# An input projection of which five indices of the convolution side are multiplied in Strassen pairs

## The chip, the cores and the metric

The kernel runs on one core of one Trainium2 chip. The metric is the time of one execution on the device in microseconds (us). Before the change it is 1025.28 us, the median of three runs (1023.85 to 1026.14).

## The reference, cut to what matters

A block with two branches that read the same normalised input (512 tokens after 16 meta tokens, 2048 wide):

```python
hn = _rmsnorm(h_res, norm_in_g[l])
P = hn @ w_in[l]                       # 2048 x (4224 + 4096)
Pr, Pc = P[..., :RW_COLS], P[..., RW_COLS:]
...
y = _rwkv7_recurrence(rh, decay, kh, vh, kk, kk * ah)      # 16 tokens, then chunks of 64
...
Bg = Pc[..., 0 * D_CONV:1 * D_CONV]
Cg = Pc[..., 1 * D_CONV:2 * D_CONV]
hc = Pc[..., 2 * D_CONV:3 * D_CONV]
g_c = Pc[..., 3 * D_CONV:4 * D_CONV]
y_b = Bg * _causal_depthwise_conv(Cg * hc, conv_w[l]) * jax.nn.silu(g_c)
mix = jnp.concatenate([y_a, y_b], axis=-1)
h_res = h_res + mix @ w_out[l]
...
out = _rmsnorm(h_res, norm_f_g)
```

All is float32. The convolution is causal, three tokens wide, so a half of the tokens needs two tokens of the half before it.

## The kernel before, in words

**Tiles.** The input projection has 65 column tiles of 128: r, k, v and g (eight indices each), one low-rank tile, and on the convolution side B, C, h and gc (eight indices each). The tokens are in the columns of the matmuls: the input stands in SBUF as `xh` and `xl`, 16 blocks of 128 rows (depth) by 528 tokens, a rounded part and its remainder. Each block of weights is split the same way, and a product is three matmuls: rounded weights by both input parts, and the weights' remainder by the rounded input (`steps`, L305 to L317). Tiles r, g, C and h are done in two banks of 258 and 256 tokens, k and v in two of 264, B and gc in one of 512.

**Weights.** A tile's weights come as two halves of 512 KB (128 by 1024, depth 0 to 1023 and 1024 to 2047). `prefetch` (L128) loads a half on SP's queue into one of three raw buffers and splits it in two quarters (`split_w`, L121): ACT casts (L124), then DVE subtracts for the even quarter and POOL for the odd one (L125). There are six buffers for quarters, so up to three halves are split ahead of PE.

**Order.** PE's order is written out by hand. The list `plan` gives the order of the projection's tiles; `mains` is a generator that yields a matmul at a time, and `fill(ns)` (L529) takes as many from it as its argument covers by their columns. The arguments are the planner's costs `FW`. The other engines' instructions are ordered by the tile framework by priority. `later(ns, fn)` holds a transfer back until so much projection has been issued.

**Stages.** For each two of the eight pairs of heads, a couple (`prepare` twice, then `invert`), PE does low-rank, Gram and inversion matmuls with `fill` between them; the inversion's small triangular solve goes through DRAM and back. Operands of the recurrence are stashed in DRAM. Then `recur` (L918) goes through nine chunks; each loads its operands (`load_chunk`, L909: eight tiles `ct` of 288 KB per chunk, two chunks buffered) and has three fills, `p`, `u` and `s`. The rest of the projection is used up by these fills and those of the mixing after them. The last stage, from about 860 us, is the output projection; it is already done in Strassen form, and there sums of weights are made by transfers that add to their destination, issued by POOL (`add_by_transfer`, L1177).

**The convolution side before.** `use` (L379) empties the banks by DVE (`scaled`, L331: product times the token's scale `rs`), multiplies C and h on POOL, convolves (ACT and DVE), multiplies by B on POOL and gates by gc.

Of the kernel before, what the change touches and what calls it, by code (L numbers as in the profile page):

```python
# [27 lines left out]
NPAIR = 8  # L28
ALPHA = -0.3032653298563167
# [14 lines left out]
    evac=34, start=1062, lora=2200, gram=8000, gram_b=13500, gram2=5500, misc=2000, v=2000, vt=1000, solve=24500, solve_first=30000,  # L44
    tr=3200, lev=3000, cp=4200, out=1500, begin=19500, p=2900, u=2900, s=5200, last=3700, mix=2600,
# [3 lines left out]
AHEAD, WEIGHTS = 6000, 3000  # L49

# [26 lines left out]
def hymba_kernel(ctx: ExitStack, tc: tile.TileContext, xt, xtok, front, w_in, w_out, pv, lup, cst, msk, gf, out):  # L77
# [16 lines left out]
    yd = dp.tile([2 * NPAIR * CH, SEQ], F32, tag="yd", name="yd", bufs=1)  # L94
    mixd = {j: dp.tile([P, SEQ], F32, tag=f"mixd{j}", name=f"mixd{j}", bufs=1) for j in range(NPAIR, KT)}

# [7 lines left out]
    stream = []  # L104
    plan = [("lora", 0), ("k", 0), ("r", 0), ("B", 0), ("v", 0), ("k", 1), ("r", 1), ("v", 1), ("g", 0), ("g", 1)]
    for j in range(0, NPAIR, 2):
        if j:
            plan += [(what, i) for i in (j, j + 1) for what in ("k", "r", "v")] + [("g", j), ("g", j + 1)]
        plan += [(what, j // 2) for what in ("C", "h", "B", "gc") if j or what != "B"]
    plan += [(what, i) for i in range(4, NPAIR) for what in ("C", "h", "B", "gc")]  # L110
    tile_of = {"r": 0, "k": 8, "v": 16, "g": 24, "lora": 32, "B": 33, "C": 41, "h": 49, "gc": 57}
    for what, i in plan:
        m = tile_of[what] + i
        stream += [w_in[m, :, 0:1024], w_in[m, :, 1024:2048]]
    stream[0:8] = [stream[j] for j in (0, 2, 4, 6, 1, 3, 5, 7)]
    N_IN = len(stream)
    stream += [w_out[0, g] for g in range(3)]
    quarters, chain, low = {}, {}, {}
    state = {"next": 0}
# [7 lines left out]

    def prefetch(upto):  # L128
        while state["next"] < min(upto, len(stream) if chain else N_IN):
            j = state["next"]  # L130
            raw = chain[j - N_IN] if j >= N_IN else wp.tile([P, 1024], F32, tag="raw", name=f"wr{j}", bufs=3)
            state["dma"] = nc.sync.dma_start(raw, stream[j]).ins
            with tc.high_priority(offset=WEIGHTS):
                for q in range(2):
                    split_w(2 * j + q, raw[:, q * 512 : (q + 1) * 512], nc.gpsimd if q and 10 < j < N_IN else nc.vector)
            state["next"] = j + 1

# [8 lines left out]
    la = xp.tile([P, 2, L], F32R, name="la")  # L146
    ones = xp.tile([P, P + 2], F32R, name="ones")
    omm = xp.tile([P, 33], F32, name="omm")
    hv = xp.tile([P, 6, 8], F32, name="hv")
    hl = cp.tile([P, 2, 8], F32, name="hl")  # L150
    smask = xp.tile([P, NCH, CH], F32, name="smask")
# [6 lines left out]
    tp = ph1.enter_context(tc.tile_pool(name="tp", bufs=1))  # L158

# [3 lines left out]
    def tm(name):  # L163
        return tp.tile([P, LP], F32, tag="tm", name=name, bufs=3)
# [4 lines left out]
    cold = tp.tile([P, 512], F32, tag="tm", name="cold", bufs=3)  # L169
# [35 lines left out]
    def load_w(n, tag):  # L205
        t = view(tag, 512)
        nc.sync.dma_start(t, stream[n][:, 512:1024])
        return t
# [113 lines left out]
    def main(j, ranges, name):  # L322
        prefetch(2 * j + 4)
        ps = banks(ranges, name, pm, "main")
        for k4 in range(4):
            if k4 == 1:
                prefetch(2 * j + 5)
            yield from steps(ps, ranges, k4, 4 * j + k4)
        return ps

# [4 lines left out]
    def shift_full(ps, m, name, dst):  # L335
        pr = tp.tile([P, L + 1], F32, tag="pr", name=f"pr_{name}", bufs=2)
        nc.gpsimd.memset(pr[:, 0:1], 0.0)
        scaled(FULL, ps, pr, -1)
        sh = tm(f"sh_{name}")[:, 0:L]
        nc.scalar.activation(sh, pr[:, 0:L], AF.Copy, scale=col(V_MU, m))  # L340
        for (a, b), d in dst:
            nc.vector.scalar_tensor_tensor(
                out=d, in0=pr[:, a + 1 : b + 1], scalar=omm[:, m : m + 1], in1=sh[:, a:b], op0=ALU.mult, op1=ALU.add
            )

    def shift_real(ps, m, name, dst):
        pr = tp.tile([P, L + 1], F32, tag="pr", name=f"pr_{name}", bufs=2)
# [10 lines left out]
    def gate(g, name):  # L358
        th = tm(f"th_{name}")[:, 0:SEQ]
# [19 lines left out]
    def use(what, i, ps):  # L379
# [18 lines left out]
        elif what == "h":  # L398
# [6 lines left out]
            cv = tp.tile([P, SEQ], F32, tag="cw", name=f"cv{i}")  # L405
# [6 lines left out]
            if i == 0:  # L412
                nc.gpsimd.tensor_tensor(out=cv, in0=cv, in1=got["B", 0], op=ALU.mult)
        elif what == "B":
            b = tm(f"b{i}")[:, 0:SEQ] if i else tp.tile([P, SEQ], F32, name="b0")
            with behind_of("split"):
                scaled(REAL, ps, b, META)
            got[what, i] = b
            if i:
# [15 lines left out]
    def token_scale_sums():  # L435
# [3 lines left out]
        var = tp.tile([P, 3, 8], F32, tag="nv", name="var0")  # L439
# [20 lines left out]
    def mains():  # L460
# [35 lines left out]
        for j in range(4, len(plan)):  # L496
            what, i = plan[j]
            rg = FULL if what in ("k", "v") else REAL if what in ("B", "gc") else TAIL
            ps = yield from main(j, rg, f"{what}{i}")
            if what == "B" and i < 4:  # L500
                state["split"] = low[4 * j + 4]
# [542 lines left out]
    ph2.close()  # L1044
    with tc.tile_pool(name="ch", bufs=1, side="right", reuse_waits="tile") as ch:
        recur(ch)

# [72 lines left out]
    prefetch(len(stream))  # L1120
# [50 lines left out]
    def request(half, k, col, g):  # L1171
        t = wp.tile([P, 1024], F32, tag="raw", name=f"wo{half}{k}{col}{g}", bufs=3)
# [323 lines left out]
```

## Time and profile before

| | |
|---|---|
| median of three runs | 1025.28 us |
| span of the profiled execution, first to last instruction | 1023.6 us |
| PE, matmul busy | 1006.6 us, 98% of the span |
| DVE, ACT, POOL busy | 67%, 38%, 27% |
| transfers | 174.82 MB, a mean of 171 GB/s |

The page gives the busy time of each engine, the span in 40 slices, the transfer queues (q1 is what SP issues, q0 what POOL issues), the chain of work that ended last, and the costliest groups of instructions. A group's row has the line, the engine, the operation, output and inputs, then the busy time and the mean ns of one, then the idle time of the engine before it and what ended it. A row of waits says who waited for whom: us in total, times, longest. Matmuls are pipelined, and each is recorded with its whole latency, so what a matmul costs PE is read from the time between starts, not from its own duration. A share of a transfer queue is the time that its packets took on 16 engines, in parts of the window.

### The profile page before, as it was taken

How to read it: one execution, taken by the hardware profiler on the slowest of the kernel's cores; microseconds unless marked ns; L12 is line 12 of the kernel's file. 1: busy time of each engine (PE TensorE's matmuls, PEld its weight loads, DVE VectorE, ACT ScalarE, POOL GpSimd, SP SyncE). 2: the span in 40 equal slices, each digit the busy share in tenths (PEclk: the TensorE clock that was granted, in tenths of full speed). 3: DMA queues.
4: the chain of work that ended last, by engine and by line, in shares of the span. 5: the costliest groups of instructions: out<-in, count | busy, mean ns of one | idle time of the engine just before them, and what ended most of it. 6: DMA issues, size and time to landing. Idle time of an engine off the chain costs nothing.

```text
span 1023.6 us, 23708 instructions
## 1 busy us (share of the span) xinstructions
PE 1006.6 (98%) x9723; PEld 919.0 (90%) x9723; DVE 686.1 (67%) x1239; ACT 393.8 (38%) x729; POOL 273.8 (27%) x292
## 2 busy tenths in 40 slices
PE   9999999999999999999999999999999999999996
PEld 8899998999988999998999998889889897787885
DVE  7677954587765569654669653244555697998787
ACT  7553423344313434322434322222222335445453
POOL 0122323233332323232322232123332332015001
PEclk9999999999999999999999999999999999999999
DMA  9526476546764364864263845867673688695754
GB/s 333 152 63 148 122 190 182 150 123 143 167 172 134 96 170 99 217 167 117 83 166 98 220 139 168 309 212 235 195 232 93 183 276 192 172 319 135 172 125 165
DMA packets 185036, 174.82 MB, mean 171 GB/s; under 512 B 121568, under 2 KB 142816, under 8 KB 184416
## 3 DMA queue, kind: packets, MB, share of 16 engines
q1 hardware_dynamic: 182336, 164.40, 55.8%
q0 software_dynamic: 2304, 8.39, 4.7%
q8 instruction: 76, 1.25, 0.5%
q10 hardware_dynamic: 288, 0.52, 0.1%
q14 instruction: 32, 0.26, 0.1%
HBM read 136.92 MB, written 36.35 MB: 169 GB/s over the span
## 4 chain that ended last, share of the span: by engine, by line
PE 68%; DVE 8%; DMA 4%; issue 2%; SPq 1%; ACT 1%; POOL 0%; DVEq 0%; ACTq 0%; POOLq 0%
PE ps_gc L314 8%; PE ps_h L314 8%; PE ps_B L314 7%; PE ps_k L314 7%; PE ps_v L314 7%; PE ps_C L314 7%; PE ps_g L314 7%; PE ps_r L314 7%; DVE ol L1193 3%; DMA wo<-in_w_out_dram 2%; PE M L1220 2%; PE g L659 1%; PE zs L984 1%; PE Q L1220 1%; DVE xb L1201 1%
## 5 line engine op out<-in xcount | busy, mean ns | idle before, releaser
L125 POOL TENSOR_TENSOR wl<-wr,wh 128x512 fp32r<-128x512 f32 x119 | 169.2, 1423 | 370.8 <-ACT wh L124 356.4
L124 ACT CAST wh<-wr 128x512 fp32r<-128x512 f32 x252 | 152.7, 618 | 294.8 <-PE ps_C L314 51.9
L125 DVE TENSOR_TENSOR wl<-wr,wh 128x512 fp32r<-128x512 f32 x133 | 100.9, 765 | 109.0 <-ACT wh L124 108.6
L314 PE MATMUL ps_k<-xh,wl 128*128 128x264 f32 x256 | 73.1, 286 | 1.1 <-DVE wl L125 1.1
L314 PE MATMUL ps_v<-xh,wh 128*128 128x264 f32 x256 | 73.0, 285 | 0.0
L314 PE MATMUL ps_h<-xh,wh 128*128 128x258 f32 (+1 forms) x256 | 72.8, 284 | 0.0
L314 PE MATMUL ps_k<-xh,wh 128*128 128x264 f32 x256 | 72.8, 284 | 0.0
L314 PE MATMUL ps_v<-xl,wh 128*128 128x264 f32 x256 | 72.7, 284 | 0.0
L314 PE MATMUL ps_v<-xh,wl 128*128 128x264 f32 x256 | 72.7, 284 | 0.0
L314 PE MATMUL ps_k<-xl,wh 128*128 128x264 f32 x256 | 72.6, 284 | 0.0
L314 PE MATMUL ps_C<-xh,wh 128*128 128x258 f32 (+1 forms) x256 | 72.6, 284 | 0.0
L314 PE MATMUL ps_h<-xh,wl 128*128 128x258 f32 (+1 forms) x256 | 72.3, 282 | 0.2 <-issue 0.2
L314 PE MATMUL ps_r<-xh,wh 128*128 128x258 f32 (+1 forms) x256 | 72.4, 283 | 0.0
L314 PE MATMUL ps_g<-xl,wh 128*128 128x258 f32 (+1 forms) x256 | 72.3, 282 | 0.0
L314 PE MATMUL ps_r<-xl,wh 128*128 128x258 f32 (+1 forms) x256 | 72.2, 282 | 0.0
L314 PE MATMUL ps_g<-xh,wl 128*128 128x258 f32 (+1 forms) x256 | 72.0, 281 | 0.0
L314 PE MATMUL ps_C<-xl,wh 128*128 128x258 f32 (+1 forms) x256 | 72.0, 281 | 0.0
L314 PE MATMUL ps_g<-xh,wh 128*128 128x258 f32 (+1 forms) x256 | 72.0, 281 | 0.0
L314 PE MATMUL ps_h<-xl,wh 128*128 128x258 f32 (+1 forms) x256 | 71.9, 281 | 0.0
L314 PE MATMUL ps_r<-xh,wl 128*128 128x258 f32 (+1 forms) x256 | 71.9, 281 | 0.0
L314 PE MATMUL ps_C<-xh,wl 128*128 128x258 f32 (+1 forms) x256 | 71.9, 281 | 0.0
L314 PE MATMUL ps_B<-xh,wl 128*128 128x512 f32 x128 | 51.3, 401 | 0.0
(353 smaller groups left out, 3006.2 us busy)
## 6 DMA issues: line engine op xcount, KB each, us to landing
wr<-in_w_in_dram SPq DMA_DIRECT2D x126, 512.0 KB
ct<-opd SPq DMA_DIRECT2D x64, 288.0 KB
wo<-in_w_out_dram SPq DMA_DIRECT2D x24, 512.0 KB
x<-in_w_out_dram POOLq DMA_DIRECT2D x16, 512.0 KB, 6.2
opd<-ar SPq DMA_DIRECT2D x8, 576.0 KB
opd<-gt SPq DMA_DIRECT2D x16, 288.0 KB
opd<-bt SPq DMA_DIRECT2D x64, 64.0 KB
x<-in_w_out_dram SPq DMA_DIRECT2D x8, 512.0 KB
```

The costliest lines, as they stand in the source:

```text
L124: nc.scalar.copy(hi, rq)
L125: low[q] = eng.tensor_tensor(out=lo, in0=rq, in1=hi.bitcast(F32), op=ALU.subtract).ins
L314: nc.tensor.matmul(ps[r], ww[:, w], xx[:, kt, a:b], start=(kt == 0 and n == 0), stop=(kt == KT - 1 and n == 2))
L659: nc.tensor.matmul(z[h][:, c - c0], bk[hs, c, h : h + 2, :].rearrange("p a s -> p (a s)"), ar[hs, c].rearrange("p a s -> p (a s)"), start= ...
L984: nc.tensor.matmul(d[hs, j], w, x[hs], start=(a == 0), stop=(a == b - 1))
L1193: nc.vector.tensor_tensor(out=lo, in0=rq, in1=hi.bitcast(F32), op=ALU.subtract)
L1201: nc.vector.tensor_tensor(out=h, in0=h, in1=ps, op=op)
L1220: nc.tensor.matmul(bank[s], left(prod, jj, m, s), w, start=(jj == 0 and n == 0), stop=(jj == 7 and n == 2))
```

## The change

For five indices i = 1 to 5 the tiles C and h form one pair (s = 0), B and gc the other (s = 1). A pair is a product of a 2 by 2 block matrix of weights (two tiles, two halves of the depth) by a 2 by 2 block matrix of inputs (two halves of the depth, two halves of the tokens). Eight block products were done; Strassen's way needs seven, M1 to M7, each 24 matmuls of 258 tokens (s = 0, both halves with two tokens before them) or 256 (s = 1).

- **Weights.** M1, M2 and M3 use a plain half. M5 and M7 use a sum of two halves: SP loads one, POOL's queue adds the other by an accumulating transfer. M6 uses a sum of three (one load, two adds, in a tile of its own); M4 adds one more to that sum. The sums are jobs (`start`) that `prefetch` begins some halves ahead when a raw buffer is free: three buffers, and two more (X3, X4) once the couples of heads are done and until the last M3.
- **Inputs.** M1, M2 and M4 use parts of `xh` and `xl`. M6, M5, M7 and M3 use sums of input blocks, made one after the other in one place, `fh` and `fl` (`form`): F6, F5, S3 and F3, in four pieces each. F6 and F3 take six DVE operations a piece, F5 and S3 four (three or two sums of inputs with both their parts, and the remainder), and one ACT cast.
- **Results.** M1 is copied by ACT, M2, M6 and M4 are added to it by DVE, and the partial sums go to DRAM (`partd`, 4 blocks of 258 per index and pair). M5 and M7 are copied by ACT and added in DRAM to two of the blocks each by an accumulating transfer of POOL's queue. For M3 the blocks are fetched back, the last sum is made and the convolution (s = 0) or the gate (s = 1) follows.
- **Order.** `plan` is written out: a digit is a product, then the index and the pair. M1, M2, M6 and M4 stand among the tiles of the head groups; all M5, then all M7, then all M3 stand after them, beside the recurrence. Indices 0, 6 and 7 stay as they were.
- **Beside it.** Some fills are larger (before each inversion 26500 for 24500, `p` and `u` 3100 for 2900, `s` 5700 for 5200) and `mix` is smaller (2100 for 2600); B0 waits in DRAM from its product to its use; some tiles move to other pools; two temporaries for three in the first stages.

The diff, cut to its core:

```diff
-    plan = [("lora", 0), ("k", 0), ("r", 0), ("B", 0), ("v", 0), ("k", 1), ("r", 1), ("v", 1), ("g", 0), ("g", 1)]
...
+SPREAD = (
+    "v0 k1 r1 F60 v1 F61 g0 F62 g1 F63 k2 110 r2 210 610 v2 410 111 k3 211 611 r3 "
+    "411 v3 120 220 g2 620 k4 420 121 221 r4 621 k5 421 130 230 v4 630 r5 430 131 v5 "
+    "231 631 g3 431 140 g4 240 640 k6 440 r6 141 241 k7 641 v6 441 150 250 r7 650 v7 "
+    "450 151 g5 251 651 g6 451 g7 C0 F5 h0 510 511 520 521 530 gc0 531 540 541 550 551 "
+    "S3 C6 710 711 720 721 730 h6 731 740 741 750 751 F3 B6 310 311 320 321 330 331 340 "
+    "341 350 351 gc6 C7 h7 B7 gc7"
+)
...
+    def start(job):
+        jobs.remove(job)
+        kind, item = job[2:]
+        if kind == "load":
+            t = started[item] = take_slot(f"wr{item}", slots_for(item))
+            state["dma"] = nc.sync.dma_start(t, halves[item]).ins
+            return
+        prod, i, s = item
+        if prod == "M6":
+            t = fp.tile([P, 1024], F32, tag="Y", name=f"y{i}{s}", bufs=2)
+            parts_ = [(0, 0), (1, 0), (1, 1)]
+        else:
+            t = take_slot(f"x{prod}{i}{s}", 5)
+            parts_ = [(1, 0), (0, 0) if prod == "M5" else (1, 1)]
+        state["dma"] = nc.sync.dma_start(t, half_of(i, s, *parts_[0])).ins
+        for p in parts_[1:]:
+            nc.gpsimd.dma_start(t, half_of(i, s, *p), accum_op=ALU.add)
+        running[item] = t
...
+    def follow(item, t):
+        if item[0] == "M6":
+            nc.gpsimd.dma_start(t, half_of(item[1], item[2], 0, 1), accum_op=ALU.add)
+            running["M4", item[1], item[2]] = t
...
+    def product_of(item, bank):
+        prod, i, s = item
+        f = form_of[item]
+        prefetch(f + 4)
+        xs = [x[:, :, 2 * s : HW] for x in LEFTS[prod]]
+        for q in range(2):
+            hi, lo = quarters[2 * f + q]
+            for k in range(4):
+                kt, w = 4 * q + k, slice(k * P, (k + 1) * P)
+                for n, (ww, x) in enumerate(((hi, xs[0]), (hi, xs[1]), (lo, xs[0]))):
+                    nc.tensor.matmul(
+                        bank, ww[:, w], x[:, kt], start=(kt == 0 and n == 0), stop=(kt == 7 and n == 2)
+                    )
+                    yield (HW - 2 * s) * 0.43
...
+    FORMS = {
+        "F6": (X01, (-1, X11), (-1, X00)), "F5": (X11, (-1, X01)), "S3": (X00, (-1, X01)),
+        "F3": ((fh, fl), (1, X11), (-1, X10)),
+    }
...
+            if prod == "M1":
+                nc.scalar.copy(t[:, 1], bank)
+            elif prod == "M2":
+                add_to(t[:, 0], t[:, 1], bank)
+                later(3500, lambda: nc.sync.dma_start(d[:, 0], t[:, 0]))
+            elif prod == "M6":
+                add_to(t[:, 1], t[:, 1], bank)
+                later(3500, lambda: nc.sync.dma_start(d[:, 2:4], t[:, 1].unsqueeze(1).to_broadcast([P, 2, n])))
+            else:
+                add_to(t[:, 0], t[:, 1], bank)
+                later(3500, lambda: nc.sync.dma_start(d[:, 1], t[:, 0]))
+                held.pop((i, s))
+            return
+        if prod in ("M5", "M7"):
...
+            nc.scalar.copy(t, bank)
+            nc.gpsimd.dma_start(
+                d[:, 2:4] if prod == "M5" else d[:, 1:4:2], t.unsqueeze(1).to_broadcast([P, 2, n]), accum_op=ALU.add
+            )
+            return
+        q = held[i, s, 1]
+        add_to(q[:, 0], q[:, 0], bank)
+        if s == 0:
+            conv(i)
+            if i != couples[-1]:
+                fetch(couples[couples.index(i) + 1])
+        else:
+            finish_couple(i)
```

278 lines of the change are left out of this document (234 added, 44 removed).

## The prediction

> **What bounds the kernel now.** I read the head of the page first, then the list of who waited for whom on PE alone, then the chain of waits in order of time, and last the transfers in short windows.
>
> ```profile
> span 1023.6 us, 23708 instructions
> PE 1006.6 (98%) x9723; PEld 919.0 (90%) x9723; DVE 686.1 (67%) x1239; ACT 393.8 (38%) x729; POOL 273.8 (27%) x292
> PEclk9999999999999999999999999999999999999999
> ```
> ```profile
> PE t L831 <- DVE xn L822: 2.2, 1, 2.2
> PE prs L454 <- POOL yb L447: 1.7, 1, 1.7
> PE pwarm L173 <- DVE cold L170: 1.4, 1, 1.4
> PE ps_k L314 <- DVE wl L125: 1.1, 1, 1.1
> ...
> PE rz L932 <- DMA ct<-opd: 0.4, 1, 0.4
> ```
>
> The second fence is PE's whole list but for three rows of 1.0 us and less: all of PE's waits together are under 9 us of 1023.6. So PE is the bound from end to end: what is taken off its stream comes off the time, and every new wait of PE is added to it. The clock was granted in full.
>
> What a tile costs on PE is read from the end of the chain, where four projection tiles run back to back:
>
> ```profile
> 810.13 11.41 PE ps_C L314 x96
> 821.54 11.41 PE ps_h L314 x96
> 832.95 11.11 PE ps_B L314 x48
> 844.06 11.14 PE ps_gc L314 x48
> ```
>
> C and h are 96 matmuls of 258 or 256 columns (257 on the mean), 118.9 ns each; B and gc are 48 of 512, 231.8 ns each. Half the columns cost 51% of the time, so cutting tiles into half-token products is nearly free of overhead.
>
> The second resource is the 16 transfer engines. The recurrence begins with a stretch in which they are full, and the output projection has one with accumulating transfers nearly alone:
>
> ```profile
> q1 hardware_dynamic: 2066, 4.66, 101.8%
> ...
> ct<-opd SPq DMA_DIRECT2D x8, 288.0 KB
> wr<-in_w_in_dram SPq DMA_DIRECT2D x2, 512.0 KB
> ```
> ```profile
> q0 software_dynamic: 268, 1.02, 90.2%
> q1 hardware_dynamic: 65, 0.22, 11.9%
> ```
>
> The first is the window from 639 to 651 us: 101.8% of 12 us for 4.66 MB, 2.62 us per MB. So a 512 KB weight half (0.524 MB) takes all 16 engines for 1.37 us, and one step of operands (eight ct of 288 KB, 2.36 MB) 6.2 us. The second is 851 to 857 us: 90.2% of 6 us for 1.02 MB, 5.3 us per MB; a 512 KB transfer that adds to its destination takes them 2.78 us, twice a plain one. The shares add up to 100% in both windows: one queue's packets take the place of the other's.
>
> **What it removes from PE.** Per index, C and h took 192 matmuls (22.82 us); seven products of 24 matmuls of 258 columns are 168 x 119.3 ns = 20.04 us, 2.78 less. B and gc took 22.25 us; 168 matmuls of 256 columns at 118.4 ns are 19.89, 2.36 less. Five indices: 25.7 us. Nothing else leaves PE's stream, and the order around it keeps PE's other work whole.
>
> **What it adds to the vector engines.**
>
> ```profile
> L125 DVE TENSOR_TENSOR wl<-wr,wh 128x512 fp32r<-128x512 f32 x133 | 100.9, 765 | 109.0 <-ACT wh L124 108.6
> L203 DVE TENSOR_TENSOR accd<-accd,sqx 128x528 f32<-128x528 f32 x15 | 10.6, 709 | 0.2
> L124 ACT CAST wh<-wr 128x512 fp32r<-128x512 f32 x252 | 152.7, 618 | 294.8 <-PE ps_C L314 51.9 <-PE ps_k L314 46.9 <-PE ps_g L314 39.2
> L125 POOL TENSOR_TENSOR wl<-wr,wh 128x512 fp32r<-128x512 f32 x119 | 169.2, 1423 | 370.8 <-ACT wh L124 356.4 <-issue 5.3 <-DMA ct<-opd 4.4
> L1178 POOL DMA_DIRECT2D x<-in_w_out_dram x16 | 14.6, 911 | 99.9 <-DVE ol L1193 92.4 <-DVE wl L125 7.5
> ```
> ```profile
> 155.00:636.00 481.00, 477.62 (x4606) 453.21 (x4605) 310.53 (x608) 168.62 (x310) 142.24 (x151) 1.00 0.56 146
> 636.00:790.00 154.00, 153.41 (x2843) 136.95 (x2843) 69.60 (x120) 41.40 (x79) 46.07 (x39) 1.00 0.69 216
> ```
>
> Ten pairs have 70 weight halves to split where they had 40: 30 more, each two ACT casts (0.618), one DVE (0.765) and one POOL subtraction (1.423): ACT 37, DVE 23, POOL 43 us. The four input forms are 80 DVE operations on 516 columns (F6 and F3 24 each, F5 and S3 16 each; I take 0.709 us from the 528-column row): 57 us. POOL issues 70 more transfers (five into weights, two into partial sums per pair) at 0.911: 64 us. Emptying the banks takes four DVE operations per pair, about as before, and three ACT copies more. The window rows (from 155 to 636 us and from 636 to 790; the columns are PE, PEld, DVE, ACT, POOL) have DVE at 65% and 45%, ACT at 35% and 27%, POOL at 30% and 30%, so on the mean this fits beside PE and costs nothing. Two places have little cover. F3 is 24 operations, 17 us of DVE; it may start only when the last M7 product has read the form it overwrites, and is covered by tile B6 alone (11.1 us and the recurrence beside it) on a DVE that has other work for 45% of the time. It could cost nothing if DVE puts it first, and 15 us if it shares evenly; I take 3. In the early stage a chained weight sum (M6) has its second accumulate waiting on POOL's queue for the first to land; behind it stand the odd quarters of weights and POOL's part of the decay path, which PE's matmuls wait for in turn.
>
> ```profile
> x<-in_w_out_dram POOLq DMA_DIRECT2D x16, 512.0 KB, 6.2
> ```
>
> One landing is 6.2 us; the weights are split up to three halves ahead, 17 us of ordinary tiles, and the fill before each inversion was made 2 us longer. Bounds for this stage: nothing, and one landing for each of four couples, 25 us. I take 2, since M6 products stand alone between whole tiles.
>
> **What it adds to the transfers.** Four plain halves per pair become three plain ones, three load-and-add sums (M6, M5, M7) with one more add each in M6 and M4: five accumulates and six plain loads. Each M5 and M7 product also adds its result to two partial sums in DRAM, 264 KB in pieces of 1 KB. No row shows an accumulate into DRAM: 0.69 us at the plain rate, 1.40 at the accumulate rate, 2.78 if a 1 KB piece costs half of a 4 KB piece; I take 1.40, the nearest row.
>
> M1, M2, M6 and M4 are spread over some 430 us of the early stage among whole tiles, where the engines stood at 0.56. Per pair they bring three plain halves, three accumulates and 0.5 MB of stores, 13.8 us, 138 in all, while 32 halves of tiles that leave this stage take 44 along: 0.2 more. They fit; tile B0's new way through DRAM (256 KB out and back) is under 2 us of them. The M5 and M7 products do not: all twenty stand in one stretch from C0 to F3, and the recurrence, which brings its operands by the same engines, starts inside it.
>
> PE's time for the stretch: C0, h0, gc0, C6, h6 56.7 us, twenty products 57.2, some 3 of the last inversion, and the recurrence. Its share comes from one step of before:
>
> ```profile
> 693.71 1.09 PE rz L932 x64
> 694.80 3.42 PE ps_C L314 x27
> 698.21 0.62 PE rz L949 x32
> 698.84 3.41 PE ps_C L314 x27
> ...
> 704.85 1.58 PE ps_C L314 x12
> 706.43 4.28 PE ps_h L314 x36
> 710.72 1.09 PE rz L932 x64
> ```
>
> A step is 17.0 us, of which projection 12.7 and recurrence 4.3. With fills of 11.9 instead of 11.0 a step carries 13.7 us of projection; counting the written fills, the recurrence starts about 3 us into gc0, so some 74 us of the stretch lie beside it, 5.4 steps, 23 us. Total: 140 us.
>
> The engines' time for it: twenty sums at 1.37 + 2.78, 83 us; twenty DRAM adds, 28; six plain halves inside and five loaded ahead for B6 and M3, 15; seven steps of operands, 43; results of the recurrence, 3. That is 172, less two sums begun before C0 (8): 164. So 24 us do not fit, and engines stand still while all slots hold finished halves (three slots before the recurrence, five in it); I put 5% for that, 8 us. **PE waits 32 us.** Bounds: with the DRAM adds at 0.69, six steps and no loading ahead, 134 us, no wait; the other way, adds at 2.78 and operands at what the whole recurrence shows,
>
> ```profile
> q1 hardware_dynamic: 25250, 30.86, 71.4%
> ...
> ct<-opd SPq DMA_DIRECT2D x54, 288.0 KB
> wr<-in_w_in_dram SPq DMA_DIRECT2D x18, 512.0 KB
> ```
>
> (640 to 776 us: 97 us, less 18 halves, is 72 for eight steps, 9 us each), 215 us, a wait of 75. The sums' slots leave no way round: a sum can begin only when the half five places ahead is split. SP's queue adds nothing of its own: a load that waits there for a slot holds the next step's operands behind it, but these are wanted a step, 17 us, later.
>
> [...]
>
> **Sum.** 1023.6 - 25.7 + 32 + 3 + 2 = 1034.9 of the profiled execution; the median shown lies 1.7 above its span, so **1037**: slower by 1.1%.
>
> **Rivals.** (1) The transfers keep up, not slower: the DRAM adds are cheap and the sums run ahead in the gaps that C0, gc0, C6 and h6 leave. For it: the row of 639 to 651 us shows the engines full without a loss of rate, and PE waited 0.4 us there. Against it: the 164 us above. With a wait of 6: 1023.6 - 25.7 + 6 + 1.7 = 1006. It decides when the stretch's transfers fall under some 145 us. (2) In between: a wait of about 20 with 3 and 2 beside it returns just what the products save: 1025. (3) The early stage waits too, each couple for a POOL queue held by a chained sum or for the inversion's round trip through DRAM: 25 us on top, 1060. Against it: four waits of PE of over 1 us in the whole run of before. (4) The products save nothing, since a half-width matmul might be held by its weight load: 1062. The four tile rows speak against it; under 1 in 50.
>
> **Chances.** Forecast (1028 to 1050) 0.48, rival 1 (1000 to 1022) 0.33, rival 2 0.07, rivals 3 and 4 0.12. A measurement of this kernel can tell about 0.2%, 2 us, from no change. Faster 0.33, same 0.07, slower 0.60. The range leaves out the best fifth or so of rival 1 and the far end of rival 3: 1005 to 1060; the forecast's own is 1028 to 1050.
>
> **What would show it.** PE's list of waits names the split weights (behind them POOL's accumulates) before products of M5 and M7, 1.5 to 7 us at a time, some 30 us together, and the slices of the recurrence show transfers at 9 with PE under 9. q0 goes from 8.39 MB to about 40, and its share from 4.7% to over 20%. PE has some 240 more matmuls in 26 us less of issue. I am wrong if PE's waits stay under 10 us (rival 1), or if they stand before F3's first products or the inversions instead. The step most likely to fail is the price of the DRAM add, and after it the count of operand steps inside the stretch.

## The result, and the profile after

The changed kernel takes 1187.9 us (median of four runs, 1184.4 to 1189.6); the kernel before, on the same chip, 1025.7 us (1023.9 to 1026.3). The ratio is 1.158, with a 95% interval of 1.156 to 1.161. The sign of the forecast holds; its size does not: 162 us slower where 12 were forecast.

The head of the page of the changed kernel:

```profile
span 1185.7 us, 24904 instructions
PE 1025.6 (86%) x9963; PEld 951.0 (80%) x9963; DVE 794.8 (67%) x1371; ACT 441.0 (37%) x835; POOL 407.3 (34%) x397
PE   9799998998979989899999648496847698799997
PEclk9899998999989999899998869898978899899998
...
q1 hardware_dynamic: 193984, 185.94, 53.4%
q0 software_dynamic: 14944, 39.87, 19.8%
```

Read two numbers against before. PE's idle time, span less busy, is 160.1 us where it was 17.0. And PE is busy for 19.0 us *more* (1025.6 for 1006.6), though its stream became shorter: that is the second row of digits, the granted clock, which was 9 from end to end and is not now. So the account of the 162.1 us between the two spans is: 25.7 less work as forecast, 143.1 more idle time, and the remainder, 44.7, put down to matmuls that run at a lower clock (its mean is 0.937 for 0.996; if the clock is either whole or half, as in the windows shown further down, that is some 149 us at half speed, for 8).

The stretches of the change, cut at tile C0 (618.93), at the start of B6 (851.60) and at the start of gc6 (948.29); columns are the window, its length, busy PE, PEld, DVE, ACT, POOL with counts, granted clock, share of the transfer engines, GB/s:

```profile
0.00:618.93 618.93, 578.09 (x5363) 559.93 (x5364) 435.15 (x860) 248.67 (x469) 221.59 (x238) 0.98 0.71 180
618.93:851.60 232.67, 166.02 (x2579) 155.19 (x2577) 91.56 (x136) 57.12 (x116) 92.54 (x80) 0.85 0.92 236
851.60:948.29 96.69, 63.81 (x994) 57.48 (x993) 71.78 (x96) 25.27 (x50) 41.02 (x32) 0.84 0.52 142
948.29:1185.70 237.41, 217.73 (x1034) 178.40 (x1032) 196.30 (x280) 109.93 (x200) 52.17 (x48) 0.97 0.72 201
```

PE idles 40.8, 66.7, 32.9 and 19.7 us in them. The second is the stretch of the twenty M5 and M7 products: 232.7 us where the forecast had 172 (140 and a wait of 32), with the transfer engines at 92%. The third, B6 and the M3 products, has the transfer engines half idle and DVE at 74%.

PE's list of waits has these at its head, in place of a list of 9 us:

```profile
PE rz L1211 <- DMA ct<-opd: 23.7, 8, 9.0
PE zs L1263 <- ACT u L1231: 22.5, 4, 10.5
PE t L1110 <- DVE xn L1101: 21.1, 4, 6.6
PE rz L1228 <- ACT pn L1219: 12.5, 2, 11.7
PE zs L1263 <- DVE u L1232: 9.6, 4, 4.3
...
PE M L473 <- ACT fh L484: 6.3, 1, 6.3
```

Of what the forecast expected here, split weights before M5 and M7, there is little (at most 4.5 us, in three waits on POOL). The waits stand at the recurrence's operands (`ct`) and small copies (`pn`, `u`), before the inversions (`xn`, 21.1 us) and before F3's first products (`fh`, 6.3 us). The last two are places that the prediction had named as signs of being wrong.

### The profile page after: what moved, and what is told of

Same layout as the page of the kernel before. It is cut to its first block, busy times and chain, and to the rows that moved or that the text cites. A ratio compares the mean times of both kernels' runs of the same rounds, so it can differ in the third digit from the quotient of the medians.

```text
span 1185.7 us, 24904 instructions
## 1 busy us (share of the span) xinstructions
PE 1025.6 (86%) x9963; PEld 951.0 (80%) x9963; DVE 794.8 (67%) x1371; ACT 441.0 (37%) x835; POOL 407.3 (34%) x397
## 4 chain that ended last, share of the span: by engine, by line
PE 20%; DMA 10%; DVE 10%; issue 7%; POOL 5%; ACT 1%; SPq 1%; DVEq 0%; POOLq 0%; ACTq 0%
PE M L1514 4%; PE P L1514 3%; DMA xM<-in_w_in_dram 3%; PE M L473 2%; POOL wl L164 2%; PE Q L1514 2%; DVE F L491 2%; DMA part<-M 2%; DMA x<-in_w_out_dram 1%; PE ps_C L436 1%; PE ps_h L436 1%; PE ps_gc L436 1%; PE ps_v L436 1%; PE ps_r L436 1%; DVE ol L1487 1%
## 5 line engine op out<-in xcount | busy, mean ns | idle before, releaser
L164 POOL TENSOR_TENSOR wl<-wr,wh 128x512 fp32r<-128x512 f32 x109 | 173.4, 1610 | 195.6 <-ACT wh L163 187.9
L163 ACT CAST wh<-wr 128x512 fp32r<-128x512 f32 x232 | 139.2, 617 | 175.0 <-PE ps_r L436 36.5
L164 DVE TENSOR_TENSOR wl<-wr,wh 128x512 fp32r<-128x512 f32 x123 | 97.5, 796 | 78.5 <-ACT wh L163 78.3
L473 PE MATMUL M<-fh,wh 128*128 128x258 f32 (+1 forms) x320 | 92.4, 289 | 8.7 <-ACT fh L484 6.3
L473 PE MATMUL M<-fh,wl 128*128 128x258 f32 (+1 forms) x320 | 92.0, 288 | 2.5 <-POOL wl L164 2.5
L473 PE MATMUL M<-fl,wh 128*128 128x258 f32 (+1 forms) x320 | 92.4, 289 | 1.0 <-DVE fl L485 0.8
L473 PE MATMUL M<-xh,wl 128*128 128x258 f32 (+1 forms) x240 | 68.4, 285 | 2.0 <-POOL wl L164 2.0
L473 PE MATMUL M<-xh,wh 128*128 128x258 f32 (+1 forms) x240 | 68.5, 286 | 0.0
L473 PE MATMUL M<-xl,wh 128*128 128x258 f32 (+1 forms) x240 | 68.5, 285 | 0.0
L473 PEld LDWEIGHTS M<-fh,wh 128*128 128x128 f32 x320 | 61.8, 193 | 7.3 <-ACT fh L484 6.8
```

Source lines behind the costliest of these rows:

```text
L163: nc.scalar.copy(hi, rq)
L164: low[q] = eng.tensor_tensor(out=lo, in0=rq, in1=hi.bitcast(F32), op=ALU.subtract).ins
L473: nc.tensor.matmul(bank, ww[:, w], x[:, kt], start=(kt == 0 and n == 0), stop=(kt == 7 and n == 2))
```

## Experiments

All ratios are to the kernel before, on the same chip; its median was 1024.2 to 1025.7 us on each of them. Four single parts of the change came first. In the expectations of the runs down to `e7_no_forms`, theory A is that the rate of the transfer engines sets the time, theory B that engines stand in order behind something that has not landed.

### The adds in DRAM

```diff
             nc.scalar.copy(t, bank)
-            nc.gpsimd.dma_start(
-                d[:, 2:4] if prod == "M5" else d[:, 1:4:2], t.unsqueeze(1).to_broadcast([P, 2, n]), accum_op=ALU.add
-            )
             return
```

> The M5 and M7 results are copied from their banks but not added into DRAM, so these terms are missing from the convolution side; all else is as in the changed kernel. The twenty adds hold the engines 1.7 us each (256 pieces at 105 ns on 16 engines), 34 us. By A the time falls by these 34 us and a little of the halved clock: 1140 to 1155. By B every wait for a landing of such an add goes, in ACT, DVE and POOL, and what stands behind: 1090 to 1130.

Measured: 1134.5 us, ratio 1.107 (1.104 to 1.110), 53 us under the changed kernel. The stretch from C0 to B6:

```profile
615.89:810.34 194.45, 158.66 (x2579) 148.74 (x2578) 93.18 (x138) 58.52 (x119) 71.56 (x62) 0.89 0.90 252
```

It is 38.2 us shorter and its transfers still fill 90%. The share times the length falls from 214 to 175 us. 18 of the adds were issued in that stretch: 2.1 us each by its length, 2.2 by the engines' time. Most of the other 15 us are in the stretch of the M3 products (87.4 us for 96.7) and before C0 (3.0). The time lies between the ranges of the two theories.

### Plain weights for M5 and M7

```diff
-            parts_ = [(1, 0), (0, 0) if prod == "M5" else (1, 1)]
+            parts_ = [(1, 0)]
```

> M5 and M7 are multiplied by one plain weight half, so the second half of their sum is missing from the output; twenty accumulating transfers of 512 KB less, 2.8 us of the engines each, 56 us. By A the time falls by about these 56 us and some clock, more than in the run without the adds into DRAM: 1110 to 1130. By B only POOL's waits for the first half to land go (26 us), not those of ACT and DVE: 1140 to 1175.

Measured: 1155.6 us, 1.128 (1.124 to 1.131). The stretch:

```profile
615.75:819.53 203.78, 160.69 (x2579) 150.79 (x2577) 86.54 (x136) 57.32 (x116) 72.97 (x60) 0.89 0.79 217
```

53 us of engine time are gone (214 to 161), but only 28.9 of the length. Here the engines are no longer full, and PE still idles 43 us: something else holds it by then. The time is in theory B's range.

These two runs also price the transfers that add, each kind alone on POOL's queue (q0), the adds in DRAM first:

```profile
q0 software_dynamic: 4624, 4.48, 15.8%
```
```profile
q0 software_dynamic: 2880, 10.49, 30.3%
```

That is 15.8% of 203.7 us for 18 adds in DRAM, 1.8 us each, and 30.3% of 194.4 us for 20 weight sums, 2.95 us each.

### Own buffers for the copies of M5 and M7

The changed kernel copies these banks to two buffers that the forms use too, and a buffer is free only when its add has landed.

```diff
-                held[prod] = two(side_tile(f"{prod}{i}"), 0)
+                if "post" in state:
+                    held[prod] = two(state["post"].tile([P, SEQ + 4], F32, tag="pq", name=f"{prod}{i}", bufs=6), 0)
+                else:
+                    held[prod] = two(side_tile(f"{prod}{i}"), 0)
```

> The copies of the M5 and M7 banks, made while the recurrence runs, go into the six buffers that M3 uses later, in place of two that they share with the input forms; no transfer, matmul or sum is changed. If the transfer engines' rate is what PE waits for (A), nothing moves: 1180 to 1190. If PE waits because ACT and DVE stand in order behind a copy or a form that waits for an add into DRAM to land (B), the recurrence's waits for u and pn (some 53 us of gaps) lose half or more and the halved clock behind them goes too: 1110 to 1150.

Measured: 1159.4 us, 1.131 (1.128 to 1.135): 28 us from buffers alone, with every transfer kept. So about half of what the adds cost is their landing time, by which a buffer and the copies behind it on ACT's queue are held. The stretch from C0 to B6 is 15.6 us shorter, with the engines at 95%:

```profile
615.00:832.09 217.09, 162.66 (x2579) 152.42 (x2578) 97.85 (x142) 59.29 (x120) 89.19 (x79) 0.87 0.95 244
```

It is what theory B names, at less than the size that B forecast (1110 to 1150). In the changed kernel this is such a copy, waiting 8.9 us for an add to land; the list of waits has six like it (ACT, M, on `part`: 30.4 us):

```profile
677.37 0.38 ACT L559 COPY M<-M 128x258 f32<-128x258 f32 x1 [8.93 <-DMA part<-M]
```

It falls into the worst of PE's gaps: the window from 675 to 700 us has PE busy for 4.09 us of 25.

### Operands first

```diff
-        load_chunk(ch, 0, range(NPAIR), ops)
-        load_chunk(ch, 1, range(NPAIR), ops)
+        with tc.high_priority(offset=CT):
+            load_chunk(ch, 0, range(NPAIR), ops)
+            load_chunk(ch, 1, range(NPAIR), ops)
```

> The operands of the first two chunks of the recurrence stand ahead of the M5 weight halves on SP's queue. No transfer is added or dropped. By A the engines are full there and the wait of 25 us before the first recurrence matmuls only moves to the weights: 1175 to 1190. By B that wait is SP's queue held by weight halves that wait for a buffer, and goes with its halved clock: 1145 to 1160.

Measured: 1188.0 us, 1.159 (1.154 to 1.164). Theory A's range holds. The waits for `ct` have shrunk from 23.7 to 0.6 us in PE's list, and the time stands one step on:

```profile
PE rz L1230 <- ACT pn L1221: 35.0, 4, 16.4
```

The row of `ct` named what ended the wait last, not what the time was spent on.

### Several parts at once, and the early stage

`e5_light_m5m7` is the first, second and fourth of these edits together.

> No adds into DRAM, plain weight halves for M5 and M7 (the missing terms are left out of the output), and the first operands ahead on SP's queue: in the M5 and M7 stretch POOL waits for no landing and the engines have 90 us less to do. The input forms and the early stage are unchanged. By A and B alike the stretch loses nearly all its waits; what stays above 1000 is then the forms' (DVE and ACT in order), the early stage's and the M3 stretch's: 1060 to 1090. If it stays above 1110, both are wrong and the products or the forms themselves are the cost.

Measured: 1099.9 us, 1.074 (1.071 to 1.077), above the 1060 to 1090 of both theories. The stretch is down to 161.4 us:

```profile
615.60:777.01 161.41, 152.32 (x2578) 144.12 (x2577) 86.08 (x138) 59.51 (x119) 54.52 (x42) 0.97 0.76 247
```

`e6_plain_m6m4` leaves the weight sums of M6 and M4 as one plain half.

```diff
-            parts_ = [(0, 0), (1, 0), (1, 1)]
+            parts_ = [(0, 0)]
...
-            nc.gpsimd.dma_start(t, half_of(item[1], item[2], 0, 1), accum_op=ALU.add)
             running["M4", item[1], item[2]] = t
```

> M6 and M4 are multiplied by one plain half (the added halves are missing from the output); the thirty accumulating transfers of the early stage go. Before 640 us PE lost 49 us in gaps against 8 in the kernel before, and some 15 more at the halved clock. If POOL, held by a chained sum, and the longer round trip of the inversions are the cause, 35 to 55 us go: 1130 to 1155. If the early gaps come from DVE's and ACT's added work, they stay: 1175 to 1188.

Measured: 1156.4 us, 1.129 (1.126 to 1.132). All of it lies before C0, which starts at 588.2 instead of 618.9 us; from there on the stretches are as in the changed kernel:

```profile
0.00:588.16 588.16, 569.16 (x5364) 552.90 (x5364) 430.72 (x860) 249.65 (x469) 192.82 (x208) 0.99 0.59 163
588.16:820.30 232.14, 167.37 (x2579) 156.50 (x2578) 90.61 (x136) 56.82 (x116) 92.14 (x80) 0.84 0.92 236
```

So the chained sums cost the early stage 30.7 us. In seven runs that change nothing made before C0 (e1, e2, e3, e4, e5, e7, e15), C0 starts at 612.4 to 617.9 us; against these the cost is 24 to 30 us.

### No forms after F6

```diff
     def form(name):
+        if name[0:2] != "F6":
+            return
```

> F5, S3 and F3 are not made, so M5, M7 and M3 are multiplied by the F6 input; all transfers stay. 56 DVE operations and 12 casts less, and none that waits for a buffer between a chunk's matmuls and the copies that PE waits for. By A (engines full) 5 to 15 us less: 1173 to 1183. By B the waits for pn and u that stand behind a form go: 1140 to 1165.

Measured: 1155.4 us, 1.128 (1.117 to 1.140). Its two executions lie 10 us apart, and the profiled one is the faster, 36.9 us shorter than that of the changed kernel. Of these, 17.8 lie between B6 and gc6, where F3 was made, and 10.7 between C0 and B6, where F5 and S3 were:

```profile
834.30:913.21 78.91, 62.63 (x995) 57.10 (x993) 55.97 (x73) 23.71 (x47) 39.64 (x31) 0.87 0.62 174
```

DVE has 23 operations and 15.8 us less there, and the stretch is shorter by 17.8: nothing covers F3. The stretch is also 9.3 us shorter in the run without the adds and 7.8 in that with own buffers, though both make F3; so these savings may overlap and are not to be added up.

### Bare

No adds in DRAM, plain weights for M4 to M7, and of the forms only F6: the order, the products and the splits of the change, almost without its transfers and forms.

> All of it together: no accumulating transfer for weights or partial sums, no F5, S3, F3; the seven products, their banks' copies, their 30 more weight halves and the order stay. The sum on PE's stream alone says 1025 - 26 = 999. If the products are as cheap as the four tile rows said, 1000 to 1025; anything above is what the order, the smaller buffers and the splits cost by themselves.

Measured: 1069.0 us, 1.044 (1.038 to 1.050). What is left is still 45 us slower than before, though PE's stream is 25.7 us shorter. The range of 1000 to 1025 was missed: without the transfers that add and the later forms, this order of work still does not pay.

### Are the fills or the smaller buffers to blame?

Both edits are made to the kernel *before*: the fills of the change, and two temporaries for three.

```diff
-    ... solve=24500, solve_first=30000,
-    ... begin=19500, p=2900, u=2900, s=5200, last=3700, mix=2600,
+    ... solve=26500, solve_first=32000,
+    ... begin=21500, p=3100, u=3100, s=5700, last=3700, mix=2100,
```

> The kernel before with nothing but the change's fills (inversions 26500 and 32000, begin 21500, p and u 3100, s 5700, mix 2100). e8_bare still lost 45 us to before with no accumulating transfer and one form left. Theory A (the loss of the bare kernel is its order: products and forms beside the engines' small work): the fills alone change nothing by more than 5 us, 1020 to 1030. Theory B (the larger fills let the recurrence run out of projection to fill with, so PE waits at its end): 1035 or more, with waits of PE before rz and zs in the last chunks.

> The kernel before with two temporaries of 2.2 KB per partition instead of three in the first stages, as the change has them. Theory A (the bare kernel's loss is its order): within 5 us of before, 1020 to 1030. Theory C (the smaller buffers chain DVE, ACT and POOL in the first stages): PE waits of 10 us and more there, 1035 to 1050.

Measured: 1027.6 us (1.0022, 1.0010 to 1.0034) and 1024.8 (1.0004, 0.9992 to 1.0015). In the kernel before, the fills cost 2 us, the buffers nothing that can be told. Theories B and C fall; that the loss is the order, theory A, is what they leave, not what they show.

### What a wait costs

In the kernel before, after C and h of seven indices, PE is made to wait for a chain of ACT copies, short or long:

```diff
+        nc.tensor.matmul(a, xh[:, 0, 0:P], xh[:, 0, 0:64], start=True, stop=True)
+        with tc.high_priority(offset=40000):
+            nc.scalar.copy(gapt, a)
+            for _ in range(10):           # 1 in the short form
+                nc.scalar.copy(gapt, gapt.bitcast(F32))
+        nc.tensor.matmul(b, xh[:, 0, 0:P], gapt, start=True, stop=True)
```

> The kernel before with 14 inserted pauses of PE, two per index after tiles C and h (not index 7): a matmul of 64 columns, two short ACT copies in a chain, and a matmul that needs the second. Each should hold PE some 1 us. Both theories: no drop of the granted clock, so the time rises by the waits' length alone, 10 to 25 us: 1035 to 1050, clock 0.99 or more.

> As the short pauses, with eleven copies in the chain instead of two, so each pause holds PE some 3 us. Theory L (a wait costs its length): the time rises over before by what the list of waits shows for PE, some 40 us, clock 0.99 or more. Theory H (a wait of over some 2 us halves the granted clock for 3.4 us or a multiple after it): 14 periods of half clock, each 1.7 us or more on top: 65 to 95 us over before, granted clock 0.95 to 0.97.

Measured: 1038.9 us (1.014, 1.011 to 1.017) and 1110.6 (1.084, 1.081 to 1.087). PE's engine row and its waits, short form first:

```profile
PE 1009.5 (97%) x9751; PEld 922.1 (89%) x9751; DVE 689.9 (67%) x1239; ACT 399.0 (38%) x757; POOL 271.6 (26%) x292
...
PE pb_h L516 <- ACT gapt L514: 6.9, 7, 1.3
PE pb_C L516 <- ACT gapt L514: 6.0, 7, 1.5
```

```profile
PE 1034.6 (93%) x9751; PEld 943.4 (85%) x9751; DVE 685.8 (62%) x1239; ACT 428.0 (39%) x883; POOL 272.9 (25%) x292
...
PE pb_h L516 <- ACT gapt L514: 35.8, 7, 5.8
PE pb_C L516 <- ACT gapt L514: 24.1, 7, 4.0
```

PE does the same 9751 matmuls in both, yet is busy 25.1 us longer in the second. Divided by the 14 long pauses, of 4.3 us on the mean and 5.8 at most, that is 1.8 us on top of a wait's length; the short ones, of 1.5 us or less, cost nothing on top (12.9 us of waits and 28 more matmuls, 13.4 us of span). Around one long pause, from 162 to 167.2 us, in the second kernel:

```profile
162.00:167.20 5.20, 0.18 (x3) 0.06 (x1) 2.44 (x4) 4.03 (x15) 2.31 (x2) 0.88 0.00 0
167.20:170.60 3.40, 3.26 (x8) 2.69 (x9) 0.69 (x1) 1.13 (x3) 3.40 (x3) 0.50 0.49 134
170.60:174.00 3.40, 3.40 (x12) 2.64 (x12) 0.00 (x0) 0.00 (x0) 0.30 (x1) 0.68 1.22 209
174.00:180.00 6.00, 6.00 (x28) 4.86 (x27) 0.00 (x0) 0.00 (x0) 0.00 (x0) 1.00 0.17 54
```

After the pause the clock is granted at half: 8 matmuls in 3.4 us, and 28 in 6 us once it is whole again. The three shares (0.88, 0.50, 0.68) add up to 6.8 us at half clock here. Over the whole execution the granted clock is 0.966 with the long pauses and 0.998 with the short ones. Theory H stands.

The kernel before has one case itself: its one wait of 2.2 us (before an inversion, in the list quoted in the prediction) ends at 306 us, and this is the next window:

```profile
306.30:309.70 3.40, 3.25 (x37) 2.75 (x38) 0.55 (x2) 2.08 (x4) 0.00 (x0) 0.51 0.89 289
```

But the same wait of 2.2 us in the run with two temporaries, which ends at 306.7 us, has none behind it, and neither has one of 2.5 us in the changed kernel (the next window, 432.8 to 436.2 us, is at 1.00):

```profile
306.70:310.10 3.40, 3.40 (x44) 2.85 (x45) 0.69 (x1) 2.11 (x4) 0.45 (x1) 1.00 0.84 261
```

So a wait of this size need not bring the half clock. In the traces of the kernel before and of the changed one, counting idle gaps of PE that began at the whole clock, a half clock began in or within 3.5 us after none of the 6 gaps of 1.1 to 1.7 us, 2 of the 5 of 2.0 to 2.5 us, and all 17 of 2.9 us and more. It lasted 3.4 us after the one wait of the kernel before (306.3 to 309.7 us), and 3.4 to 30.7 us at a time in the changed kernel, the longest (674.2 to 704.9 us) with four more gaps inside it.

### Which queue holds PE?

Every split's subtraction on DVE, none behind POOL's waits for landings; then the same in the kernel before:

```diff
-        low[q] = eng.tensor_tensor(out=lo, ...
+        low[q] = nc.vector.tensor_tensor(out=lo, ...
```

> The changed kernel with every subtraction of a split made by DVE, none by POOL, so that none stands in POOL's queue behind an accumulate that waits for a landing. Theory Q (POOL's queue, held by landings, is what holds the splits and through them PE): 30 us or more faster than the changed kernel, 1158 or less. Theory R (DVE is the queue in which the recurrence's copies are late, and 150 more operations of 0.77 us make it worse): 1190 to 1230.

> The control: the kernel before with every subtraction of a split made by DVE. Without accumulates POOL's queue holds nothing up, so only DVE's load changes (67% to about 76%). Both theories: 1025 to 1040; if it is 1050 or more, DVE's load alone makes waits even in the kernel before, and e13 must be read against that.

Measured: 1167.1 us (1.138, 1.135 to 1.142), 21 us under the changed kernel, and 1024.3 (0.999, 0.998 to 1.001) for the control. Neither theory's number: what the edit takes away cost something, not most of it. Most of the 21 us lie before C0, which starts at 604.9 us, for 612.4 to 618.9 where that stage is left alone. But the edit did a second thing. With POOL's subtractions gone, DVE's own operations took less time (a subtraction 0.70 us for 0.80, F's sums 0.69 for 0.80), so DVE did 149 operations more in 5 us more of busy time (800.1 for 794.8). How much of the gain is POOL's queue and how much DVE's shorter operations stays open. For the same reason the control raised DVE's load only to 70%, not to 76%: it shows that 25 us more on DVE cost nothing there, not that DVE's load never counts.

`e15_own_ct_first` joins the own buffers and the early operands, with all transfers kept; `e16_bare_ct_first` is the bare kernel with early operands.

> The changed kernel with all its transfers and products, with own buffers for the bank copies of M5 and M7 in the recurrence and with the operands of the first two chunks loaded early. Alone the first gave 28 us and the second none. Theory H (the late operands stood in front of other waits, each hiding the other): together 45 us or more, 1143 or less. Theory S (what ends the waits is the engines' queues at that point, whatever the operands): 1155 to 1165, with ACT's pn and u copies in place of ct in PE's list.

> e8_bare (no accumulates into weights or DRAM, one form; so it leaves parts of the sums out) with the operands of the first two chunks loaded early. Theory H: the ct waits (8.6 us) and the half clock behind them go, 1052 to 1060. Theory S: other waits take their place, 1064 to 1072. In neither case does it come under before, 1025.

Measured: 1167.4 us (1.139, 1.134 to 1.143) and 1067.1 (1.041, 1.037 to 1.044). Theory H falls in both, and theory S's ranges hold but for 2 us: taking away the wait for operands moves the wait and saves nothing (e15 is 8 us slower than own buffers alone, e16 2 us faster than the bare kernel). The chain of e16 shows three products back to back, and its stretch from C0 to B6 what is left without the transfers that add:

```profile
292.36 8.52 PE M L473 x72
```

```profile
593.13:751.79 158.66, 150.83 (x2579) 142.81 (x2577) 74.05 (x122) 57.44 (x115) 54.19 (x42) 0.98 0.75 245
```

### The inversions' round trip

Before the inversions PE waits 21.1 us although the fill there is longer. SP's issues in the last couple, changed kernel first (ACT had copied the norms `n` at 581.1), then the kernel before (566.9):

```profile
583.11 1.31 SPq L1052 DMA_DIRECT2D xT<-sx  x1
...
586.54 0.44 SPq L878 DMA_DIRECT2D sn<-n  x1
...
591.58 0.33 SPq L878 DMA_DIRECT2D nd<-sn  x1
```

```profile
567.33 0.26 SPq L599 DMA_DIRECT2D sn<-n  x1
...
569.02 0.55 SPq L599 DMA_DIRECT2D nd<-sn  x1
```

The trip starts 5.4 us after the copy instead of 0.4, behind the other pair's loads, and its first leg takes 5.0 us instead of 1.7. So the trip was put on ACT's queue:

```diff
+    act = nc.scalar.dma_start
...
-            behind(rows(sg, h), gt[64 * h : 64 * h + 64, h, :, 0:CH])
+            act(rows(sg, h), gt[64 * h : 64 * h + 64, h, :, 0:CH])
```

and likewise the norms' store, the two loads, the small solve's store and the inverse's loads.

> The changed kernel with the inversion's round trip through DRAM (stores of norms and Gram blocks, their loads, the store of the small solve, the loads of the inverse) issued on ACT's queue instead of SP's. Theory Q (SP's in-order queue makes the trip late): PE's waits before the inversions fall from 21.1 to under 8 us and the time by 15 us or more, 1173 or less. Theory D (DVE's load makes the small solve late): the waits stay at 15 us or more, 1180 to 1200.

> e16_bare_ct_first (no accumulates, one form; parts of the sums are left out) with the same move to ACT's queue. Theory Q: PE's waits before the inversions fall from 11.9 to under 4 us, 1048 to 1058. Theory D: they stay at 9 us or more, 1062 to 1075.

Measured: 1187.4 us (1.159, 1.153 to 1.164) and 1065.5 (1.040, 1.028 to 1.051). The waits did what theory Q said (4.3 us left in the changed kernel, none in the bare one), and the time did not:

```profile
PE t L1110 <- DVE xn L1101: 4.3, 1, 4.3
```

That row had 21.1. Yet PE idles as long before C0 as in the changed kernel, and C0 comes 7 us later:

```profile
0.00:626.04 626.04, 583.37 (x5363) 565.80 (x5364) 436.53 (x860) 247.91 (x469) 223.45 (x238) 0.96 0.69 177
```

Splits on ACT stand now behind the trip's issues, which wait for the data that they store; of ACT's list of waits in the same run:

```profile
ACT wh L163 <- DVE y L1046: 26.6, 4, 11.6
```

So SP's order was the cause of that row, and the move gained nothing. Whether SP's order costs time by itself stays open, since the move made ACT hold the casts in its place.

## Why the prediction failed in size

**PE's stream: right.** Three products take 8.52 us, 2.84 each; seventy by that row are 198.8 us for the 225.4 of the removed tiles, 26.6 less where 25.7 were forecast. By the account above, what ate it is PE's waits and its clock.

**The transfers of the stretch: the mechanism right in part, the term too small.** The forecast had the engines full in the stretch from C0 on, and they are. It had PE wait there for the split weights of M5 and M7, and PE hardly does: it waits mainly for operands and small copies, and own buffers took 15.6 us off the stretch with every transfer kept. The forecast had 164 us of engine time there; the trace has the following in the 232.5 us from 619.0 to 851.5:

```profile
q1 hardware_dynamic: 28009, 39.54, 52.5%
q0 software_dynamic: 7504, 14.96, 39.3%
...
ct<-opd SPq DMA_DIRECT2D x60, 288.0 KB
xM<-in_w_in_dram POOLq DMA_DIRECT2D x20, 512.0 KB, 7.1
```

That is 122.1 us for q1 and 91.4 for q0, 213.5 together. The forecast's terms, sorted in the same way, were 88 and 84, less 8 for sums begun before C0. None was: all twenty adds are in the window (8 us). q1 took 3.09 us per MB where the window of before that I priced by gave 2.62: at that price its 39.54 MB are 18.5 us dearer. Neither full engines nor transfers that add explain this price. Without any transfer that adds, and with the engines at 75%, it is 3.07 (`e5_light_m5m7`, 615.6 to 777 us):

```profile
q1 hardware_dynamic: 28033, 39.46, 75.0%
```

And the prediction's own row of 640 to 776 us, before the change, has it at 3.15 (71.4% of 136 us for 30.86 MB). The window of 639 to 651 us held only operands and weight halves, 2.3 KB a packet on the mean; the longer one and the stretch hold the recurrence's small transfers too, 1.2 and 1.4 KB a packet. So the price was read from a window that was not like the stretch. q1's bytes are 5.6 MB more than my terms held (33.9), half a step of operands (sixty tiles are seven and a half), partial sums fetched back and stores: 15 us. And a DRAM add cost 1.8 us where I took 1.40, a weight sum 2.95 where I took 2.78: with 18 of the adds for 20, 8 us. The total comes near the outer bound that I had worked out, 215 us and a wait of 75, but by other terms, so that is luck. The stretch was 61 us longer than the 172 forecast. Both of the steps that I had called likeliest to fail, the price of the DRAM add and the count of operand steps, did, by a few us each; the price per MB weighed more than either.

**The early stage: rival 3's term, taken at 2 us.** It costs 30.7 us (C0 at 618.9 against 588.2), its bound was 25. The mean share of the transfer engines was the wrong thing to read for it, for they stood at 0.71 there and were not full: the sums are chained in time, and POOL's queue holds what stands behind them. Taking POOL's subtractions away brought C0 7 to 14 us forward, which fits this but does not prove it, since DVE's operations were shorter too.

**F3: taken at 3 us, measured 17.8**, about its full time on DVE (15.8 us less there without it). The outer bound of 15 assumed that DVE would share; in that stretch DVE is at 74% with the gates and convolutions of five indices, and every us goes through.

**Every wait was added at its length.** That was the error common to all terms. The long pauses, 4.3 us on the mean, cost 1.8 us more each; in the changed kernel the account above puts 44.7 us down to the lower clock. The one case in the kernel before is too short to show in 40 slices of the clock, by which I had called it granted in full.

**"On the mean this fits beside PE and costs nothing": the step that failed for the rest.** The added casts, subtractions, bank copies and sums were set against the mean idle time of DVE, ACT and POOL, and given no price but F3's. The bare kernel keeps these, but for the later forms, with no transfer that adds, and takes 68 us more than PE's stream alone would (a span of 1066.2 in e16 for 1023.6 - 25.7): 47 more of idle PE, 21 of lower clock.

**"SP's queue adds nothing of its own": not borne out, but its price is not shown either.** SP held both the operands and the inversions' trip. Both waits could be taken away (early operands, ACT's queue), and both times the time stayed, with other waits in their place. A wait that heads PE's list is worth what its removal gives, and that had to be measured.

Over the forecast's 1034.9 the profiled execution is 150.8 us long. Of these, the early stage is 28.7, the stretch 60.7 and F3 14.8: 104. The other 47 are about what the bare kernel's 68 us leave when the 19 us of the stretch that are no transfers (158.7 us there against my 140) are taken off. The bare kernel has PE waiting before the inversions, at a bank that DVE empties late, at the recurrence's copies and at the hand-over to the output projection; the first rows of its list (of e16):

```profile
PE t L1109 <- DVE xn L1100: 11.9, 4, 4.7
PE M L1514 <- ACT wh L164: 8.4, 1, 8.4
PE ps_k L436 <- DVE pr_g L599: 5.0, 1, 5.0
PE rz L1263 <- DVE u L1232: 4.8, 1, 4.8
```

The 21 us of lower clock (0.976 on the mean in e16) are put down to such waits, as in the long pauses. Fills and buffers cost 2 us at most in the kernel before, early operands gained the bare kernel 2 us, and moving the trip off SP's queue 2 more, within the noise. What is left is that more splits, bank copies and sums stand on the in-order queues between PE's dependent steps (DVE 744 us for 686 in the whole run, POOL 336 for 274). That is argued, not shown: no run takes away the splits alone. Longer operations on DVE are not it, for its subtractions take 0.77 us on the mean in e16 as in the kernel before. No version tried came under the kernel before; with the sums left out and only one form, it was 41 us above it.

## What to carry to other kernels

Where PE is at 98% with hand-written fills, work that it saves is worth its length, but work that others get is not covered by their mean idle time: price it where it stands, by what is chained to it. Price transfers by a window that holds the same mix of them. Count transfers that add, and the landing time for which they hold a buffer, before counting matmuls saved: here 26 us of PE were bought with 53 us of DRAM adds and 64 of weight sums (32 for M5 and M7, 32 for M6 and M4), each taken away alone. And add to each new wait of PE of some 3 us or more the half clock behind it, about 1.8 us each in the long pauses here.

## What the runs showed of the hardware

With 14 waits of PE of 4.3 us on the mean (e12) the granted clock was 0.966, with 14 of up to 1.5 us (e11) 0.998. In the traces of before and after a half clock began in or within 3.5 us after all 17 gaps of 2.9 us and more, and after 2 of the 5 of 2.0 to 2.5 us. DVE's subtractions of 128 by 512 took 0.80 us beside POOL's in the changed kernel and 0.70 with none on POOL (e13). A transfer that adds to DRAM in pieces of 1 KB took the engines 1.8 us for 258 KB (e4), longer per byte than one that adds to SBUF in whole halves (2.95 us for 512 KB in the same stretch of e3), and held its source until it landed, 6.9 us later in the changed kernel:

```profile
part<-M POOLq DMA_DIRECT2D x9, 258.0 KB, 6.9
```
